# RMSNorm with swish on one core: 88 rows loaded ahead of the first store and 8 behind it, in place of 80 and 16

## The chip, the core and the metric

The kernel runs on one core of a Trainium2 chip. The time is what the device takes for one execution, in microseconds. Before the change it is 159.97 us, the median of 3 runs (159.83 to 160.32). The profile was taken in a run of 159.75 us, of which the profiled span, from the first instruction to the last landing, is 158.4 us.

## What is computed

The input is 16 x 1024 rows of 512 float32 numbers, 33.55 MB, and the output is as large. Each row is divided by its root mean square, multiplied by gamma, and put through the swish function:

```
rms = np.sqrt(np.mean(x ** 2, axis=-1, keepdims=True) + eps)
x_norm = x / rms * gamma
return (x_norm * (1.0 / (1.0 + np.exp(-x_norm)))).astype(np.float32)
```

## The kernel before

**Rows and groups.** Each of the 128 partitions handles 128 rows of 2 KB. In what follows "row" means such a row on every partition at once, so one row is 128 x 2 KB = 256 KB of traffic, and 128 rows are loaded and 128 stored. `groups = [32, 48, 16, 32]` says how rows are laid on the tensor in HBM: in a group of n rows every partition has n rows in one contiguous piece, so partitions lie n x 2 KB apart (64, 96, 32 and 64 KB). No load or store crosses a group's end.

**The ring.** `xb` holds 96 rows on each partition. Rows 0 to 95 have a place of their own; rows 96 to 127 reuse the places of rows 0 to 31, so their loads need the store of rows 0 to 31 to have landed. Everything is computed in place in `xb`.

**Loads and stores.** `loads` and `stores` are lists of (first row, number of rows), one DMA each. All are issued by SP (SyncE) on one hardware queue, which spreads each DMA over the core's 16 DMA engines, 8 partitions on each. `order` is the order in which SP issues them, written out by hand:

- loads at rows 0, 4, 8, then gamma, then loads at 16, 24, 32, 48, 64 (11 rows) and 75 (5 rows);
- `("landed", 64)`: SP waits until the load of rows 64 to 74 has landed (line 166);
- the store of rows 0 to 31, which itself waits for the swish of its four units (`s_swish`, lines 117 to 123), then the load of rows 80 to 95;
- `("stored", 0)`: SP waits until the store of rows 0 to 31 has landed, then issues the loads at 96, 112 (13 rows) and 125 (3 rows);
- `("landed", 112)`, then the stores at 32, 64, 80, 96 and 120, each on its swish.

**Compute.** Rows are worked in 16 units of 8 rows. ScalarE (ACT) squares and sums six rows of a unit (line 215), VectorE (DVE) the other two (line 251), GpSimd (POOL) turns the sums into 1/rms (lines 183 and 189), DVE scales the rows by it and by gamma (line 260), and ACT applies the swish to the whole unit in one instruction (line 225, and line 245 for the last two units). ACT's loop squares unit i + 2 and then does the swish of unit i, so a unit's swish waits behind the squares of a unit two later. TensorE multiplies nothing; its queue only passes on "this unit's load has landed" to ACT (`s_land`).

Of the kernel before, what the change touches and what calls it, by code (L numbers as in the profile page):

```python
# [9 lines left out]
def kernel(  # L10
# [14 lines left out]
    of = out.flatten_outer_dims()  # L25
    R, D = xf.shape

    groups = [32, 48, 16, 32]
    ring = 96
    loads = [(0, 4), (4, 4), (8, 8), (16, 8), (24, 8), (32, 16), (48, 16), (64, 11), (75, 5)]  # L30
    loads += [(80, 16), (96, 16), (112, 13), (125, 3)]
    stores = [(0, 32), (32, 32), (64, 16), (80, 16), (96, 24), (120, 8)]
    order = [("load", a) for a in (0, 4, 8)] + [("gamma", 0)]
    order += [("load", a) for a in (16, 24, 32, 48, 64, 75)]
    order += [("landed", 64), ("store", 0), ("load", 80)]
    order += [("stored", 0), ("load", 96), ("load", 112), ("load", 125)]
    order += [("landed", 112)] + [("store", a) for a in (32, 64, 80, 96, 120)]
    early = 2
    cn = 8
    own = 2  # L40
# [285 lines left out]
```

## Time and profile before

| What | Value |
|---|---|
| median of 3 runs | 159.97 us (159.83 to 160.32) |
| the profiled run | 159.75 us |
| its span | 158.4 us |
| traffic | 67.12 MB, 424 GB/s over the span |
| busy: ACT, DVE, POOL | 73%, 68%, 27% of the span |

The next table has all DMAs of `xb` in the order in which SP issued them: when SP issued each, when the last of its 16 engines had landed it (the issue plus the time to landing that the trace gives for it), and how long that is after the landing of the DMA ahead of it. All times are us from the span's start. Since the DMAs of the one queue land in order of issue, the last column is what each costs in line.

| DMA (rows) | issued | landed | after the one ahead |
|---|---|---|---|
| load 0 to 3 (4) | 0.00 | 4.95 | |
| load 4 to 7 (4) | 0.44 | 7.43 | 2.48 |
| load 8 to 15 (8), and gamma | 1.92 | 12.34 | 4.91 |
| load 16 to 23 (8) | 3.17 | 17.23 | 4.89 |
| load 24 to 31 (8) | 3.61 | 22.12 | 4.89 |
| load 32 to 47 (16) | 4.17 | 31.83 | 9.71 |
| load 48 to 63 (16) | 4.65 | 41.55 | 9.72 |
| load 64 to 74 (11) | 5.13 | 48.25 | 6.70 |
| load 75 to 79 (5) | 5.66 | 51.33 | 3.08 |
| store 0 to 31 (32) | 48.37 | 70.98 | 19.65 |
| load 80 to 95 (16) | 48.77 | 80.80 | 9.82 |
| load 96 to 111 (16) | 71.00 | 90.51 | 9.71 |
| load 112 to 124 (13) | 71.37 | 98.42 | 7.91 |
| load 125 to 127 (3) | 71.86 | 100.28 | 1.86 |
| store 32 to 63 (32) | 98.48 | 119.62 | 19.34 |
| store 64 to 79 (16) | 98.87 | 129.31 | 9.69 |
| store 80 to 95 (16) | 109.83 | 139.02 | 9.71 |
| store 96 to 119 (24) | 131.11 | 153.50 | 14.48 |
| store 120 to 127 (8) | 136.41 | 158.35 | 4.85 |

The landing of the last store is the end of the span.

### The profile page before, as it was taken

What the parts mean: (1) busy time and instruction counts of PE and PEld (TensorE: products, weight loads), DVE (VectorE), ACT (ScalarE), POOL (GpSimd) and SP (SyncE); (2) the same over time, 40 slices, a digit from 0 to 9 for tenths busy, and PEclk for the clock granted to TensorE, in tenths of its full rate; (3) what the DMA queues carried; (4) which work ended last, traced back from release to release, by engine and by line L of the source; (5) the groups of instructions that cost most, each with busy time, mean ns of one, the idle gap of its engine ahead of it and who ended that gap; (6) DMA issues with size and microseconds to landing.
All of it is one profiled execution on the core that took longest, in us unless ns stands there. A gap on an engine that the chain in (4) does not pass through costs nothing. (4 is left out here: it accounts for less than half of the span.)

```text
span 158.4 us, 844 instructions
## 1 busy us (share of the span) xinstructions
DVE 107.7 (68%) x198; ACT 115.7 (73%) x205; POOL 42.9 (27%) x38
## 2 busy tenths in 40 slices
DVE  0051899798989889898925989989898995000000
ACT  3608389999999999999459999999999385400000
POOL 1031426060524426060601433516061500000000
DMA  7999999999999979799999999996969999999997
GB/s 257 451 416 443 422 488 439 397 406 497 389 395 565 463 331 530 314 381 480 406 406 472 399 430 400 550 513 281 530 298 488 406 397 455 538 397 397 397 397 331
DMA packets 2744, 67.12 MB, mean 424 GB/s; under 512 B 308, under 2 KB 308, under 8 KB 440
## 3 DMA queue, kind: packets, MB, share of 16 engines
q1 hardware_dynamic: 2744, 67.12, 99.1%
HBM read 33.56 MB, written 33.55 MB: 424 GB/s over the span
## 5 line engine op out<-in xcount | busy, mean ns | idle before, releaser
L260 DVE SCALAR_TENSOR_TENSOR xb<-xb,rstd,gamma_sb 128x512 f32 (+1 forms) x128 | 86.1, 745 | 0.0
L215 ACT ACTIVATE junk<-xb 128x512 f32 (+1 forms) x94 | 54.6, 581 | 13.1 <-ACTq L98 11.3
L225 ACT ACTIVATE xb<-xb x14 | 50.5, 3604 | 0.7 <-ACTq L98 0.7
L251 DVE SCALAR_TENSOR_TENSOR junk_v<-xb 128x512 f32 (+1 forms) x34 | 22.1, 689 | 23.0 <-DVEq L98 23.0
L189 POOL TENSOR_TENSOR rstd<-aeps,neg_half 128x8 f32<-128x8 f32 x16 | 31.7, 1984 | 1.3
L183 POOL TENSOR_SCALAR aeps<-ms 128x8 f32<-128x8 f32 x16 | 10.4, 648 | 79.1 <-DVE junk_v L251 79.1
L215 ACT ACTIVATION_READ_ACCUMULATOR junk<-xb 128x1 f32 x94 | 17.7, 188 | 0.0
L245 ACT ACTIVATE xb<-xb 128x4096 f32<-128x4096 f32 x2 | 7.2, 3616 | 5.0 <-DVE xb L260 5.0
L251 DVE DVE_READ_ACCUMULATOR junk_v<-xb 128x1 f32 x34 | 2.8, 82 | 0.0
L227 ACT ACT_TABLE_LOAD x1 | 1.3, 1283 | 1.9 <-PEq L62 1.9
L269 DVE LOAD_MASK_SELECT gamma_sb<-gamma x1 | 0.0, 14 | 2.0 <-DMA gamma<-in_gamma_dram 2.0
L178 POOL MEMSET gamma<- 128x512 f32 x1 | 0.5, 524 | 1.5 <-POOLq L62 1.5
L269 DVE STREAM_SHUFFLE gamma_sb<-gamma 128x512 f32<-128x512 f32 x1 | 0.7, 719 | 0.0
L307 POOL MEMSET const-float32-0.0<- 128x1 f32 x1 | 0.1, 98 | 0.2 <-issue 0.2
L179 POOL MEMSET neg_half<- 128x8 f32 x1 | 0.1, 104 | 0.0
L307 POOL MEMSET const-bfloat16-1.0<- 128x1 bf16 x1 | 0.1, 103 | 0.0
L307 POOL MEMSET const-uint8-127<- 128x1 uint8 x1 | 0.1, 102 | 0.0
L307 POOL MEMSET const-float32-1.0<- 128x1 f32 x1 | 0.1, 99 | 0.0
## 6 DMA issues: line engine op xcount, KB each, us to landing
xb<-in_x_dram SPq DMA_DIRECT2D x4, 4096.0 KB, 29.9
out_dram<-xb SPq DMA_DIRECT2D x2, 4096.0 KB, 29.8
xb<-in_x_dram SPq DMA_DIRECT2D x3, 2048.0 KB, 14.1
out_dram<-xb SPq DMA_DIRECT2D x1, 6144.0 KB, 22.4
xb<-in_x_dram SPq DMA_DIRECT2D x1, 3328.0 KB, 27.0
xb<-in_x_dram SPq DMA_DIRECT2D x1, 2816.0 KB, 43.1
xb<-in_x_dram SPq DMA_DIRECT2D x2, 1024.0 KB, 6.0
out_dram<-xb SPq DMA_DIRECT2D x1, 2048.0 KB, 21.9
```

What stands on the lines that cost most here:

```text
L178: nc.gpsimd.memset(gamma4, 0.0).then_inc(s_zero, 1)
L179: nc.gpsimd.memset(neg_half, -0.5).then_inc(s_half, 1)
L183: nc.gpsimd.tensor_scalar(out=aeps[k % 2], in0=ms[min(k, 1)], scalar1=eps_f, scalar2=None, op0=ALU.add,),
L189: nc.gpsimd.tensor_tensor(out=rstd[:, k * cn : (k + 1) * cn], in0=aeps[k % 2], in1=neg_half, op=ALU.pow),
L215: nc.scalar.activation(out=dummies[j], in_=rows[j], func=AF.Square, scale=inv_d**0.5, accum_out=sums[:, j : j + 1],)
L225: nc.scalar.activation(out=rows, in_=rows, func=AF.Silu).then_inc(s_swish, 1)
L227: nc.scalar.preload_act_table_set("silu_and_others")
L245: nc.scalar.activation(out=rows, in_=rows, func=AF.Silu), s_norm, n + 1
L251: ins = nc.vector.scalar_tensor_tensor(out=junk_v[j], in0=rows[j], scalar=inv_d, in1=rows[j], op0=ALU.mult, op1=ALU.mult, accum_out=to[:, ...
L260: ins = nc.vector.scalar_tensor_tensor(out=rows[j], in0=rows[j], scalar=factors[j], in1=gamma_sb, op0=ALU.mult, op1=ALU.mult,)
L269: need(nc.vector.stream_shuffle(gamma_sb, gamma4, [0] * 32), s_gld, 16).then_inc(s_gamma, 1)
L307: nc = _bacc.Bacc("TRN2", target_bir_lowering=False, num_devices=1)
```

## The change

The groups become groups of 32, 56, 8 and 32 rows, so that partitions lie 64, 112, 16 and 64 KB apart. The two loads of rows 64 to 74 and 75 to 79 and the first half of the load of rows 80 to 95 become one load of 24 rows, 64 to 87; rows 88 to 95 are a load of 8 rows. The two stores of rows 64 to 79 and 80 to 95 become stores of 24 and 8 rows. SP no longer waits for the load at row 64 before the first store; the load behind that store is that of rows 88 to 95. There is one load fewer and the same number of stores. The instruction lists of DVE, ACT, POOL and TensorE are the same as before.

```
-    groups = [32, 48, 16, 32]
+    groups = [32, 56, 8, 32]
     ring = 96
-    loads = [(0, 4), (4, 4), (8, 8), (16, 8), (24, 8), (32, 16), (48, 16), (64, 11), (75, 5)]
-    loads += [(80, 16), (96, 16), (112, 13), (125, 3)]
-    stores = [(0, 32), (32, 32), (64, 16), (80, 16), (96, 24), (120, 8)]
+    loads = [(0, 4), (4, 4), (8, 8), (16, 8), (24, 8), (32, 16), (48, 16), (64, 24)]
+    loads += [(88, 8), (96, 16), (112, 13), (125, 3)]
+    stores = [(0, 32), (32, 32), (64, 24), (88, 8), (96, 24), (120, 8)]
     order = [("load", a) for a in (0, 4, 8)] + [("gamma", 0)]
-    order += [("load", a) for a in (16, 24, 32, 48, 64, 75)]
-    order += [("landed", 64), ("store", 0), ("load", 80)]
+    order += [("load", a) for a in (16, 24, 32, 48, 64)]
+    order += [("store", 0), ("load", 88)]
     order += [("stored", 0), ("load", 96), ("load", 112), ("load", 125)]
-    order += [("landed", 112)] + [("store", a) for a in (32, 64, 80, 96, 120)]
+    order += [("landed", 112)] + [("store", a) for a in (32, 64, 88, 96, 120)]
```

## The prediction

> **What bounds the kernel now.** I read the page's busy shares and DMA queue first, then SP's waits, then SP's and ACT's timelines around the first store, and last the time from issue to landing of each DMA (the table above).
>
> ```profile
> span 158.4 us, 844 instructions
> DVE 107.7 (68%) x198; ACT 115.7 (73%) x205; POOL 42.9 (27%) x38
> q1 hardware_dynamic: 2744, 67.12, 99.1%
> ```
>
> No compute engine is busy for three quarters of the span, while the packets of the one DMA queue fill 99.1% of all 16 DMA engines' time. The DMA queue is the bound, and the order of its DMAs is a line in which only two things can cost time: what each DMA takes in line, and a moment in which the line is empty.
>
> What a DMA takes in line is in the table's last column. A 16-row load takes 9.72 us, an 8-row load 4.89. Two of 8 cost 9.78, so one DMA more costs 9.78 - 9.72 = 0.06 us, and a row (9.72 - 0.06) / 16 = 0.604 us. A check with rows not used for this: 5 rows should take 0.06 + 5 x 0.604 = 3.08 (measured 3.08), 11 rows 6.70 (6.70), 24 rows 14.56 (14.48, a store). A change of direction costs a little more: store 0 took 19.65 against 19.34 for the other 32-row store, and the load behind it 9.82 against 9.72.
>
> Where the line could run empty is where SP waits with little queued. These are SP's waits:
>
> ```profile
> engine line waited for: us in total, times, longest us
> SPq L166 <- DMA xb<-in_x_dram: 68.3, 2, 42.1
> SPq L121 <- ACT xb L245: 25.9, 2, 20.9
> SPq L115 <- DMA out_dram<-xb: 21.8, 1, 21.8
> SPq L170 <- DMA out_dram<-xb: 21.6, 1, 21.6
> SPq L121 <- ACT xb L225: 10.5, 1, 10.5
> ```
>
> The two waits of line 166 are for the loads at rows 64 and 112; line 115's 21.8 us is the load at 96 waiting for store 0. Around them SP and ACT did this (start, duration):
>
> ```profile
> 3.17 2.94 SPq L115 DMA_DIRECT2D xb<-in_x_dram  x6
> 48.37 0.35 SPq L121 DMA_DIRECT2D out_dram<-xb  x1
> 48.77 23.53 SPq L115 DMA_DIRECT2D xb<-in_x_dram  x4
> 98.48 38.26 SPq L121 DMA_DIRECT2D out_dram<-xb  x5
> ...
> 44.75 3.60 ACT L225 ACTIVATE xb<-xb  x1
> 73.48 3.61 ACT L225 ACTIVATE xb<-xb  x1
> 80.96 0.60 ACT L215 ACTIVATE junk<-xb 128x512 f32 x1 [3.88 <-ACTq L98]
> 127.46 3.62 ACT L245 ACTIVATE xb<-xb 128x4096 f32<-128x4096 f32 x1 [3.30 <-DVE xb L260]
> ```
>
> I call the work still in line at an issue its cover (landing of the last DMA queued ahead, less the issue):
>
> - store 0: issued 48.37, load 75 lands 51.33: cover 2.96 us.
> - load 96: issued 71.00, load 80 lands 80.80: cover 9.80.
> - store 32: issued 98.48, load 125 lands 100.28: cover 1.80.
> - stores 64, 80, 96, 120: covers from 7.9 (131.11 to 139.02) to 29 us.
>
> The shortest cover, 1.80 us, still let store 32 take 19.34 in line, the shorter of the two 32-row stores. So no cover here has been short enough to add to the last landing.
>
> **The wait removed, and the store.** Unit 3's swish ends at 44.75 + 3.60 = 48.35; load 64 has landed at 48.25. Both end within 0.1 us and the swish is the later, so without the landed wait store 0 is still issued at 48.37. The removal alone is worth 0.0 us (at most 0.1 either way). Behind it on SP stand only the load at 88 and the loads of the ring's second round, which wait for the store's landing in any case.
>
> **Fewer loads in line.** Loads of rows 64 to 95 cost 6.70 + 3.08 + 9.82 = 19.60 us in line. Afterwards: 24 rows 0.06 + 24 x 0.604 = 14.56, and 8 rows behind a store 4.89 + 0.10 = 4.99, together 19.55. That is -0.05 us, one DMA fewer.
>
> **The stores re-cut.** 16 + 16 rows took 9.69 + 9.71 = 19.40; 24 + 8 rows, by the rows of stores 96 and 120, take 14.48 + 4.85 = 19.33. The number of DMAs is the same, so I take between 0 and -0.07: -0.03.
>
> **The two covers that move.** Load 64 (24 rows) lands at 41.55 + 14.56 = 56.11, so store 0's cover grows to 56.11 - 48.37 = 7.74 us. Store 0 lands at 56.11 + 19.65 = 75.76. Then SP issues load 96, with load 88 in line until 75.76 + 4.99 = 80.75: cover 4.99 us, where it was 9.80. What it needs: the very first load was issued into an empty line and landed 4.95 us later, of which 4 x 0.604 + 0.06 = 2.48 are transfer, so 2.47 are issue, start and landing receipt. 4.99 is twice that, and 2.8 times the 1.80 that sufficed at store 32: 0.0 us. If that cover did fail wholly, load 96 would take the 4.95 - 2.48 = 2.47 us more.
>
> The Trainium skill (DMA: Bandwidth & Descriptors, "Anatomy of one DMA") speaks against this edit: a DMA has about 2 us of fixed cost, mostly the receipt that the last byte has landed, slowest for writes to HBM. Store 0's receipt and load 96's first byte (0.6 us there) would by it use an estimated 2.6 of the 4.99 us. The line would still not run empty and the sum would be the same, but less would be to spare than the 1.80 at store 32 suggests.
>
> **Landed 112, and the compute.** Up to the load at 112 as many rows are in line as before (157), so store 32 is issued some 0.05 us earlier, with the same 1.8 us of cover. ACT no longer idles 3.88 us before unit 10, which now lands at 56.11; unit 11 lands at 80.75 and is wanted at 73.48 + 3.61 + 7.18 = 84.3 (7.18 is ACT's beat: 44.75 less 37.57, the starts of two swishes). From there ACT runs 3.9 us ahead of before: unit 10's swish ends at 98.6 (it was 102.6), unit 11's at 105.8, and stores 96 and 120 are issued at some 127 and 132.5. The line is then full for 12 us and more, so the gain ends in longer cover: 0.0 us. Were that cover gone, the end would follow ACT's last swish, which is now the earlier one.
>
> **The new layout.** Partitions lie 112 and 16 KB apart, which the trace does not show. At 96 KB (load 48) 16 rows took 9.72, at 64 KB (load 96) 9.71, at 32 KB (store 80) 9.71. I take 0.0; both bounds are by these rows: none gains over 9.69, so 0.1 us below; above, the worst difference among them, 0.1 per DMA, in 4 DMAs: 0.4 us.
>
> **Sum.** -0.05 - 0.03 = -0.08 us on a run of 159.75 us, so 159.67; the median of the runs shown lies 0.22 above the profiled run, so 159.9 us. About 0.3% (0.48 us) is what a measurement of this kernel can tell from no change, so this is no change.
>
> **Rival 1: load 96 comes too late (slower).** The place is SP's wait for store 0, the mechanism the cover of 8 rows. It decides once the time from store 0's last landing to load 96's first data exceeds what load 88 still has in line. The price is at most 2.47 us, halfway 1.2: 159.9 + 1.2 = 161.1. Against it stand the 1.80 us that sufficed at 98.48; for it, that the cover is halved and that all 16 engines must have landed the store first. Chance 0.08.
>
> **Rival 2: rows 64 to 95 move more slowly (slower).** 24-row pieces at 112 KB or 8-row pieces at 16 KB could suit HBM less, in two loads and two stores. To show, 64 rows (38.7 us in line) would need 1.3% more; at 2% it is 0.8 us: 160.7. For it there is only that no row has this layout; against it, three layouts within 0.1%. Chance 0.11.
>
> **Rival 3: the line runs empty before, in runs that were not profiled (faster).** Store 0's 2.96 us of cover hang on two events that fall within 0.1 us, and the runs spread over 0.49 us. If the median run loses 0.5 there and the new 7.74 us take that away, it is 159.4. Against it: the profiled run is within 0.14% of the median. Chance 0.13.
>
> The Trainium skill (SBUF — State Buffer, "The DMA setup-cost knee") has a rule that ends here too: some 2 us for every DMA, so one DMA fewer would give an estimated 157.9. The trace has 0.06 us between DMAs queued behind each other, so this has next to no part in the 0.13.
>
> **Chances and range.** No change 0.68; faster by over 0.3% 0.13; slower 0.19 (0.08 + 0.11). The range runs from rival 3's time with 0.1 to spare, 159.3, past rival 2's 160.7 to 160.8; rival 1's full price is left out.
>
> **What would show it.** In the profile after: store 0 issued at 48.4, landing near 75.8; load 96 issued just behind it and landing 9.7 us after load 88; ACT without a wait of over 1 us between 73 and 84; stores 24 and 8 taking 14.5 and 4.85 in line; a span of 158.3. A landing of load 96 more than 10 us behind load 88 would be rival 1; 24 rows over 14.7 us or 8 over 5.1 rival 2. An unchanged profile with a median below 159.5 would be rival 3.

## The result, and the profile after

| | before | after |
|---|---|---|
| median of 16 runs | 159.78 us | 160.37 us |
| lowest and highest | 159.53 to 160.32 | 160.04 to 160.72 |
| span of the profiled run | 158.4 us | 159.0 us |
| ratio of the times | | 1.0037, 95% interval 1.0028 to 1.0047 |

The change makes the kernel slower by 0.37%, about 0.6 us, just beyond what a measurement of it can tell from no change. The forecast was no change, 159.9 us.

The page of the changed kernel still shows a full DMA queue and compute engines with time to spare:

```profile
span 159.0 us, 842 instructions
DVE 107.7 (68%) x198; ACT 115.6 (73%) x205; POOL 42.8 (27%) x38
q1 hardware_dynamic: 2600, 67.12, 99.0%
```

The busy share of the queue does not show the loss: a packet that takes longer counts as busy. SP's timeline (start, duration):

```profile
3.17 2.36 SPq L115 DMA_DIRECT2D xb<-in_x_dram  x5
48.32 0.35 SPq L121 DMA_DIRECT2D out_dram<-xb  x1
48.71 28.98 SPq L115 DMA_DIRECT2D xb<-in_x_dram  x4
99.03 33.67 SPq L121 DMA_DIRECT2D out_dram<-xb  x5
```

The first store goes out at 48.32, as it did (48.37), but its turn in line is later. The second store goes out 0.55 us later than before (98.48). What lies between is read from the DMA issues (DMA, number, size, time from issue to landing):

```profile
xb<-in_x_dram SPq DMA_DIRECT2D x1, 6144.0 KB, 51.8
xb<-in_x_dram SPq DMA_DIRECT2D x1, 3328.0 KB, 22.2
xb<-in_x_dram SPq DMA_DIRECT2D x1, 768.0 KB, 23.5
```

The 6144 KB are the load of 24 rows: issued at 5.05, landed at 56.90. Put beside the table of the kernel before (last landings, us; only the rows around the change; the last column has the prediction's prices, and those of the kernel before where it gave none):

| DMA (rows) | issued | landed | after the one ahead | forecast |
|---|---|---|---|---|
| load 48 to 63 (16) | 4.57 | 41.50 | 9.70 | 9.72 |
| load 64 to 87 (24) | 5.05 | 56.90 | **15.40** | 14.56 |
| store 0 to 31 (32) | 48.32 | 76.40 | 19.50 | 19.65 |
| load 88 to 95 (8) | 48.71 | 81.32 | 4.92 | 4.99 |
| load 96 to 111 (16) | 76.42 | 91.03 | 9.71 | 9.71 |
| load 112 to 124 (13) | 76.79 | 98.94 | 7.91 | 7.91 |
| load 125 to 127 (3) | 77.26 | 100.80 | 1.86 | 1.86 |
| store 32 to 63 (32) | 99.03 | 120.19 | 19.39 | 19.34 |
| store 64 to 87 (24) | 99.41 | 134.76 | 14.57 | 14.48 |
| store 88 to 95 (8) | 105.78 | 139.59 | 4.83 | 4.85 |

One line is off: the load ahead of the first store takes 0.84 us too long. The DMA packets show where. Each engine moves this load in eight packets of 48 KB; seven take 1.82 us, and the eighth of all 16 engines, started between 53.2 and 53.8, takes 2.3 to 3.1 us. Nothing is idle then; the loads run slower for the last stretch ahead of the store.

### The profile page after: what moved, and what is told of

It is laid out like the page before. It is cut to its first block, busy times and chain, and to the rows that moved or that the text cites. A ratio compares the mean times of both kernels' runs of the same rounds, so it can differ in the third digit from the quotient of the medians.

```text
span 159.0 us, 842 instructions
## 1 busy us (share of the span) xinstructions
DVE 107.7 (68%) x198; ACT 115.6 (73%) x205; POOL 42.8 (27%) x38
## 5 line engine op out<-in xcount | busy, mean ns | idle before, releaser
L215 ACT ACTIVATE junk<-xb 128x512 f32 (+1 forms) x94 | 55.4, 589 | 9.1 <-ACTq L98 7.4
L215 ACT ACTIVATION_READ_ACCUMULATOR junk<-xb 128x1 f32 x94 | 18.5, 197 | 0.0
## 6 DMA issues: line engine op xcount, KB each, us to landing
xb<-in_x_dram SPq DMA_DIRECT2D x1, 6144.0 KB, 51.8
```

The costliest lines, as they stand in the source:

```text
L215: nc.scalar.activation(out=dummies[j], in_=rows[j], func=AF.Square, scale=inv_d**0.5, accum_out=sums[:, j : j + 1],)
```

## The experiments

Two numbers describe each run. The **cover** is what the first store has in line ahead of it when it is issued, at full speed (last landing of the load at 48, plus the in-line price of what follows, less the issue). The **loss** is what a stretch takes above its price in line (0.06 us for a DMA and 0.604 for a row), read from the mean landing of the 16 engines in the trace, since the last engine alone strays, by half a us in most runs and by up to 1.1: **ahead** for the loads from row 64 up to the store, **behind** for the first store and the load behind it. Each is of one profiled execution; the ratios are of the medians against the kernel before, with their 95% intervals. In some runs the profiled execution is not a typical one: it is 0.26 to 0.42 us slower than the median in b1, c3, c4, d3 and e2, and 0.31 faster in d4.

| run | store out | cover | loss ahead | loss behind | ratio |
|---|---|---|---|---|---|
| before | 48.37 | 2.96 | 0.0 | 0.15 | 1 |
| after | 48.32 | 7.74 | 0.76 | 0.08 | 1.0037 (1.0028 to 1.0047) |
| a1_tail5 | 48.26 | 7.78 | 0.66 | 0.03 | 1.0040 (1.0024 to 1.0055) |
| a2_layout64 | 48.15 | 7.74 | 0.80 | 0.0 | 1.0026 (1.0016 to 1.0037) |
| a3_before_one16 | 48.16 | 2.90 | 0.0 | 0.32 | 1.0011 (0.9998 to 1.0024) |
| a4_before_nowait | 48.25 | 2.96 | 0.0 | 0.10 | 1.0005 (0.9996 to 1.0014) |
| b1_tail5_landed | 52.91 | 2.98 | 0.08 | 0.06 | 0.9992 (0.9984 to 1.0001) |
| b2_tail10_landed | 49.88 | 6.03 | 0.84 | 0.04 | 1.0039 (1.0026 to 1.0052) |
| b3_tail8_landed | 51.00 | 4.82 | 0.99 | 0.09 | 1.0053 (1.0036 to 1.0069) |
| b4_behind_late | 48.00 | 7.75 | 1.04 | 0.0 | 1.0042 (1.0030 to 1.0054) |
| c1_store8first | 48.35 | 7.68 | 0.91 | 0.0 | 1.0034 (1.0022 to 1.0046) |
| c2_store2first | 48.25 | 7.69 | 0.77 | 0.03 | 1.0030 (1.0018 to 1.0042) |
| c4_tail3_landed | 54.20 | 1.81 | 0.0 | 0.75 | 1.0028 (1.0018 to 1.0038) |
| d4_tail7_landed | 51.80 | 4.23 | 0.50 | 0.07 | 1.0050 (1.0037 to 1.0062) |
| e1_before_early24 | 40.95 | 10.13 | 0.48 | 0.0 | 1.0019 (1.0010 to 1.0028) |
| e2_late_by_sum | 53.46 | 2.53 | 0.0 | 0.73 | 1.0016 (1.0007 to 1.0025) |

c3, d1, d2 and d3 are told below.

**First theory: the size of the last packets.** In the kernel before, the last load ahead of the store has packets of 10 KB; after, 48 KB.

a1_tail5, against after:

```diff
-    loads = [..., (48, 16), (64, 24)]
+    loads = [..., (48, 16), (64, 19), (83, 5)]
```

> The changed kernel with its load of 24 rows cut into 19 and 5 rows, nothing else. Theory T (the last packet of each engine ahead of the first store is slowed in proportion to its size, 0.91 us per engine for 48 KB packets, none for 10 KB): the time goes back to about 159.75 (ratio to before 0.999 to 1.001), and the DMA ahead of the store takes its 3.08 us in line. Theory Q (the store costs because it is issued 7.7 us ahead of its turn): no change against the changed kernel, ratio 1.0035 to 1.004, the loss now in the 5-row load or the 19-row load. Theory L (the layout with 112 KB pitch): also 1.0035 to 1.004.

1.0040. The size of the last packets is not it: the 10 KB packets are slow too. Theory T falls.

a2_layout64, against after:

```diff
-    groups = [32, 56, 8, 32]
+    groups = [32, 64, 32]
```

> The changed kernel's DMAs with groups of 32, 64 and 32 rows, so that partitions lie 128 KB apart in the third of the rows where it was 112 and 16 KB. T and Q: as the changed kernel, ratio to before 1.0035 to 1.004, with the load of 24 rows taking some 15.4 us in line. L: a different loss, below 1.002 or above 1.006.

1.0026, and the load of 24 rows took 15.61 us in line. The ratio is a little under the range of T and Q, but the loss is in the same place and of the same size with partitions 128 KB apart. The 112 and 16 KB are not needed for it.

a3_before_one16, against before:

```diff
-    loads = [..., (48, 16), (64, 11), (75, 5)]
+    loads = [..., (48, 16), (64, 16)]
...
-    order += [("landed", 64), ("store", 0), ("load", 80)]
+    order += [("store", 0), ("load", 80)]
```

> The kernel before with its two loads of 11 and 5 rows as one of 16, and so without the landed wait ahead of the first store; the store still goes out on its swish at 48.4. T: the last packets are of 32 KB, so a loss of about two thirds of 0.9 us in that load's landing, less what comes back behind the store: ratio 1.002 to 1.004. Q: the store is queued 2.9 us ahead as before, so no loss, ratio 0.999 to 1.001. L: no loss, 0.999 to 1.001.

1.0011 with an interval that holds 1, and no loss ahead of the store: the 16 rows took 9.72. This too speaks against T; the 0.3 us at the store's end is told of below.

a4_before_nowait, against before:

```diff
-    order += [("landed", 64), ("store", 0), ("load", 80)]
+    order += [("store", 0), ("load", 80)]
```

> The kernel before without the landed wait ahead of the first store, nothing else. T, Q and L alike: the store goes out on its swish at 48.4 as before, ratio 0.999 to 1.001. If the wait itself matters (a store put in line while the load of 11 rows is still landing), 1.002 or more.

1.0005, the same. In the kernel before, the wait itself is worth nothing, because the swish holds the store back as long.

**Second theory: the time at which the store is issued.** a1 cuts the stretch finely enough to see it in the windows view. The columns are the stretch, its length, busy times of DVE, ACT and POOL, the clock, the DMA share and the GB/s of the packets that start in it. a1_tail5:

```profile
53.50:54.00 0.50, 0.50 (x2) 0.50 (x1) 0.50 (x1) 1.00 1.10 348
54.00:54.50 0.50, 0.50 (x2) 0.50 (x1) 0.42 (x2) 1.00 1.38 328
54.50:55.00 0.50, 0.50 (x2) 0.50 (x1) 0.50 (x1) 1.00 0.78 184
```

The same stretch of b1_tail5_landed, which has the same DMAs and issues the store 4.65 us later:

```profile
53.50:54.00 0.50, 0.50 (x2) 0.50 (x1) 0.48 (x1) 1.00 0.98 410
54.00:54.50 0.50, 0.50 (x2) 0.50 (x1) 0.44 (x1) 1.00 0.97 389
54.50:55.00 0.50, 0.50 (x2) 0.50 (x1) 0.50 (x1) 1.00 1.02 430
```

The compute engines do the same work in both; the loads fall to 184 GB/s in one and hold 389 to 430 in the other. By the packets' own times, the loads of a1 run at some 0.55 of full speed between 54.3 and 55.2, before any packet of the store starts (the first at 55.8).

b1_tail5_landed, b2_tail10_landed and b3_tail8_landed, against after (19 and 5 rows shown; the others 14 and 10, 16 and 8):

```diff
-    loads = [..., (48, 16), (64, 24)]
+    loads = [..., (48, 16), (64, 19), (83, 5)]
...
-    order += [("store", 0), ("load", 88)]
+    order += [("landed", 64), ("store", 0), ("load", 88)]
```

> The changed kernel with loads of 19 and 5 rows in place of 24 and a landed wait for the load of 19 rows ahead of the first store: the store goes out at about 53.0 with 3.1 us of loads in line, where it went out at 48.3. Base: the same cut without the wait lost 0.64 us in line in the 5-row load (3.72 us in place of 3.08), its packets slow from 53.1 to 55.4. Theory I (loads are slowed some 4.8 us after a store was issued): the slow stretch falls at 57.8, where no load is in line, so no loss, ratio to before 0.999 to 1.001. Theory P (in the last 3 us ahead of the store's turn the engines already work on the store, if it is in line by then): it comes into line at 54, so half the loss or less, ratio 1.001 to 1.002. Theory N (the time of issue does not matter): 1.004.

> As the run with 19 and 5 rows and the wait, cut into 14 and 10 rows: the store goes out at about 50.1 with 6.1 us in line. I: the slow stretch starts at 54.9, part of the loss (0.2 to 0.5 us in the 10-row load), ratio 1.001 to 1.003. P: whole loss, slow from 53.1 to 55.4, ratio 1.004. N: 1.004.

> As the run with 19 and 5 rows and the wait, cut into 16 and 8 rows: the store goes out at about 51.2 with 4.9 us in line. I: the slow stretch starts at 56.0, when the loads are over, so no loss, ratio 0.999 to 1.001. P: whole loss, slow from 53.1 to 55.4, ratio 1.004. N: 1.004.

0.9992, 1.0039 and 1.0053. SP's timeline of b1:

```profile
52.91 0.35 SPq L120 DMA_DIRECT2D out_dram<-xb  x1
53.30 23.83 SPq L114 DMA_DIRECT2D xb<-in_x_dram  x4
```

With the store issued at 52.91 (cover 2.98) the loss is all but gone from 15 of the 16 engines; one engine still lands the 5 rows 0.6 us late, in a profile that is among the slowest of this kernel's runs (159.87, median 159.61), and why is not known. At 49.88 and 51.00 the loss is whole and begins at 53 as in the changed kernel. So it does not follow the issue at a fixed distance (theory I falls), and the issue matters (N falls). P fits best: the slow stretch lies in the last 3 us ahead of the store's turn, if the store is in line by then. Its forecast for b1, up to half the loss and 1.001 to 1.002, was missed all the same: next to nothing was lost.

b4_behind_late, against after:

```diff
-    order += [("store", 0), ("load", 88)]
+    order += [("store", 0), ("swished", 5), ("load", 88)]
...
+        elif what == "swished":
+            nc.sync.wait_ge(s_swish, a)
```

> The changed kernel with SP waiting for the swish of unit 4 (about 55.5) between the first store and the load of rows 88 to 95, so that only the store is in line behind the loads when they are slowed. I, P and N: as the changed kernel, ratio 1.0035 to 1.004, the load of 24 rows taking 15.4 us. If it is the load behind the store that disturbs the loads ahead: no loss there (14.55 us), ratio 0.999 to 1.001.

1.0042, with the loss ahead: it is the store in line that matters, not the load behind it.

c1_store8first and c2_store2first, against after (c1; c2 has 2 and 30 rows):

```diff
-    stores = [(0, 32), (32, 32), ...
+    stores = [(0, 8), (8, 24), (32, 32), ...
...
-    order += [("store", 0), ("load", 88)]
+    order += [("swished", 4), ("store", 0), ("store", 8), ("load", 88)]
```

> The changed kernel with its first store cut into 8 and 24 rows, both issued on the swish of unit 3 at 48.3 as before; SP then waits for both before the load at 96. Theory P1 (ahead of the store's turn the engines work on the store's first packet only, so the loads are at half rate for as long as that packet takes): the first packets are of 16 KB in place of 64, the stretch 0.6 us in place of 2.4, the load of 24 rows takes 14.56 + 0.23 = 14.8 us in line, ratio to before 1.0005 to 1.0015. Theory P2 (a given time or number of bytes ahead, whatever the packets): 15.4 us in line, ratio 1.004.

> As the run with 8 and 24 rows, with the first store cut into 2 and 30 rows, so first packets of 4 KB and 60 KB behind them. P1: next to no loss, 14.6 us in line for the load of 24 rows, ratio 0.9995 to 1.001. P2: 15.4 us, ratio 1.004 to 1.005.

1.0034 and 1.0030, with 15.57 and 15.38 us in line for the load of 24 rows: the loss does not depend on the first store's packets. P1 falls.

c3_before_no112, against before:

```diff
-    order += [("landed", 112)] + [("store", a) for a in (32, 64, 80, 96, 120)]
+    order += [("store", a) for a in (32, 64, 80, 96, 120)]
```

> The kernel before without the landed wait for the load at 112, nothing else: the 32-row store of rows 32 to 63 goes out at about 77 in place of 98.5, some 22 us ahead of its turn. If what was seen at the first store holds for any store in line behind loads (P1 and P2): the loads at 112 and 125 together take 0.6 to 1.0 us more than 9.76, ratio 1.003 to 1.006. If it is something of the first store alone: ratio 0.998 to 1.000, since the short idle time of the engines at 99 goes too.

1.0056 (1.0030 to 1.0083). The second store goes out at 76.85, some 22 us earlier than before, and the loads of 13 and 3 rows ahead of it lose 0.45 us in the mean and 1.2 on the last engine. The load of 3 rows landed 28.4 us after its issue before; now:

```profile
xb<-in_x_dram SPq DMA_DIRECT2D x1, 768.0 KB, 29.6
```

So the loss is not of the first store alone, and it shows what the wait for the load at 112 is worth in the kernel before: about 0.9 us.

**The time of issue alone.** In e2 all DMAs and their order are those of the changed kernel; SP waits for a count of DVE's that comes at 53.45. Against after:

```diff
-    order += [("store", 0), ("load", 88)]
+    order += [("summed", 7), ("store", 0), ("load", 88)]
...
+        elif what == "summed":
+            nc.sync.wait_ge(s_sum, a)
```

> The changed kernel with its DMAs as they are, in the same order; SP only waits, ahead of the first store, until DVE has the sums of unit 6, at about 53.45, so the store goes out at 53.5 with 2.6 us in line in place of 48.3 with 7.7. If the time of issue alone causes the loss: the load of 24 rows takes 14.5 to 14.6 us in line in place of 15.4, ratio to before 0.999 to 1.001 (up to 1.003 if the loss comes back behind the store, as with loads of 21 and 3 rows). If the single load of 24 rows takes part: 15.0 us or more, ratio 1.003 to 1.004.

SP's timeline of e2_late_by_sum, and then its load of 24 rows among the DMA issues:

```profile
53.46 0.35 SPq L120 DMA_DIRECT2D out_dram<-xb  x1
53.85 23.19 SPq L114 DMA_DIRECT2D xb<-in_x_dram  x4
```

```profile
xb<-in_x_dram SPq DMA_DIRECT2D x1, 6144.0 KB, 50.9
```

It lands 50.9 us after its issue in place of 51.8, 14.53 in line, the forecast price. The time of the store's issue alone made the difference ahead of it (the load at 88 goes out later too, but b4, with that load late and the store early, kept the loss). The time gains only part of that (1.0016): 0.73 us are lost behind the store, in a profile that is the slowest of e2's runs (160.53, median 160.11).

The two columns of loss do not add up to the time, because what the engines lie apart costs again later. In e2 the first and the last engine land the load at 88 1.57 us apart (0.92 in before). The second store is issued when all 16 have landed the load at 112, and those ahead run out of packets before its own come: by the packets' times the engines are busy for 0.4 of the time between 99.50 and 100.25, and the second store takes 0.50 us above its price in the mean, against 0.10 in before.

e1 does the reverse to the kernel before: it lets a part of the first store go out early.

```diff
-    stores = [(0, 32), (32, 32), ...
+    stores = [(0, 24), (24, 8), (32, 32), ...
...
-    order += [("landed", 64), ("store", 0), ("load", 80)]
+    order += [("store", 0), ("store", 24), ("load", 80)]
```

> The kernel before with its first store cut into 24 and 8 rows and no landed wait: the 24 rows go out on the swish of unit 2 at 41.2, 9 us ahead of their turn at 50.3, the loads and their cut (80 and 16 rows) as before. If the time of issue causes the loss: the loads of 11 and 5 rows lose 0.6 to 1.0 us between 47 and 50, ratio to before 1.003 to 1.005. If the cut into 88 and 8 rows is needed for it: 0.999 to 1.001.

1.0019 (1.0010 to 1.0028). The loads of 11 and 5 rows lose 0.48 us, between 49 and 51, ahead of a turn that lies 5 us earlier than in the changed kernel, and with the old cut into 80 and 16 rows. The ratio is under the range expected: the loss is smaller than the 0.6 to 1.0 us forecast, and the 0.15 us that the kernel before loses behind the store is not lost here.

**Where it sets in, and what comes back behind the store.** c4 and d4 differ from b1 in the rows of the last load ahead of the store, 3 and 7 in place of 5, and so in the cover.

> The changed kernel with loads of 21 and 3 rows in place of 24 and a landed wait for the load of 21 rows, so that the first store goes out at about 54.2 with 1.9 us in line, as the second store does with the loads of 13 and 3 rows. P1 and P2: no loss but up to 0.2 us of idle engines, ratio to before 0.998 to 1.000. If the idle time counts in full on the slowest engine: 1.001.

> The changed kernel with loads of 17 and 7 rows and a landed wait for the load of 17 rows: the store goes out at about 51.9 with 4.3 us in line, between the runs with 3.1 to 3.6 us (no loss) and 4.9 to 5.6 us (whole loss). If the loss sets in at once: ratio 1.004 or 0.999. If it grows with the cover: 1.001 to 1.003.

d4 (cover 4.23) loses 0.50 us ahead in its profile, the fastest of its six runs (160.07, median 160.38); by the ratio, 1.0050, a usual run of it loses as much as the kernels with longer covers. So the loss sets in between covers of 3.0 and 4.2 us (the expectation counts some of the covers larger; by the table's definition the runs on either side have 2.9 to 3.0 and 4.8 or more). c4 (cover 1.81) loses nothing ahead and 0.75 behind, 1.0028, which was not expected. Its last 64 KB packets of the store and the first packets of the load behind it are slow, as in e2.

The last attempt was to issue the loads behind the store late, too. d1 (on b1), d2 (on before) and d3 (on c4) cut the first store into 28 and 4 rows; SP waits for the 28, issues the loads at 88 (d2: 80) and 96, waits for the 4 and goes on:

```diff
-    stores = [(0, 32), (32, 32), ...
+    stores = [(0, 28), (28, 4), (32, 32), ...
...
+    order += [("landed", 64), ("store", 0), ("store", 28), ("stored", 0)]
+    order += [("load", a) for a in (88, 96)]
+    order += [("stored", 28), ("load", 112), ("load", 125), ("landed", 112)]
```

> The changed kernel with loads of 19 and 5 rows and the landed wait ahead of the first store (which alone gave ratio 0.9992), and the first store cut into 28 and 4 rows: the loads at 88 and 96 are issued when the 28 rows have landed, some 2.4 us ahead of their turn, in place of 22 us ahead. Theory S (the loss is the same for loads in line behind a store): the last packets of the store and the first of the load run at full rate, 0.15 us gained, 0.06 lost by one DMA more, ratio 0.998 to 0.9995. Theory O (only stores behind loads do this): ratio 0.999 to 1.0005.

> The kernel before with its first store cut into 28 and 4 rows and the loads at 80 and 96 issued when the 28 rows have landed. S: the 0.3 us that it loses around the end of the store are gone, less 0.06 for one DMA more: ratio 0.998 to 0.999. O: 1.000 to 1.001.

> The kernel with loads of 21 and 3 rows (ratio 1.0028, 0.8 us lost around the end of the first store, where its 64 KB packets starting at 72 took 0.59 us longer per engine) with the store cut into 28 and 4 rows and the loads at 88 and 96 issued when the 28 rows have landed. S: those 0.8 us are gone, ratio 0.998 to 0.9995. O: 1.002 to 1.004.

1.0060 (1.0043 to 1.0076), 1.0013 (1.0005 to 1.0022) and 1.0062 (1.0044 to 1.0081). Theory S falls: holding the loads back makes it worse, with losses behind the store of 0.57, 0.38 and 0.77 us and the last engine 1.2 to 1.8 us behind the first. Theory O fits d2 alone; d1 and d3 lie above its ranges as well. A store in line early slows the loads ahead of it; no run shows that a load in line early does the same to the store ahead of it.

## Why the prediction failed

**The step that failed** is the one on the covers that move: "Load 64 (24 rows) lands at 41.55 + 14.56 = 56.11, so store 0's cover grows to 56.11 - 48.37 = 7.74 us", entered in the sum with no price of its own. The cover did grow to 7.7 us, and that was the cost: the load of 24 rows took 15.40 us in line in place of 14.56, and 14.53 in e2, where the cover is 2.5 us. The step asked how short a cover may be and never whether it may be too long. The trace of before could have raised the question. Both of its stores behind loads had 1.8 and 3.0 us of cover; nothing in it showed a store that had been in line for longer with loads ahead of it, so that longer cover is free was an assumption with no row under it, and no bound was set for it.

**The wait removed.** "The removal alone is worth 0.0 us" is right of the kernel before (a4: 1.0005, interval from 0.9996). It was priced there and carried over to a line whose turn had moved by 5 us. In the new order the same wait, with a load to wait for that leaves 3 us, is worth the difference between a1 and b1, which differ in nothing else: 1.0040 and 0.9992.

**What held.** The store went out at 48.32 (forecast 48.37). Load 96 was issued 0.02 us behind the store's landing and landed 9.71 us behind load 88, so rival 1, too short a cover there, did not happen; the 5 us sufficed. The receipt of some 2 us that the prediction weighed took less: store 0's landings are counted some 0.7 us after the ends of its last packets. ACT's wait of 3.88 us is gone, and stores 96 and 120 went out at 127.06 and 132.36 (forecast 127 and 132.5) without any gain, since the line was full. Here is ACT after unit 7's swish, in the timeline, with no idle time in brackets:

```profile
73.41 3.62 ACT L225 ACTIVATE xb<-xb  x1
76.92 0.60 ACT L215 ACTIVATE junk<-xb 128x512 f32 x1
```

The stores re-cut took 14.57 + 4.83 = 19.40 us, as the two of 16 rows had; the gain of 0.03 entered for them was not there.

**Two readings that were off.** Neither moved the forecast. The covers of the last four stores reach 20.75 us (store 64: 98.87 to 119.62), not 29. And the prediction put the 19.65 us of store 0 against the 19.34 of store 32 down to a change of direction, but both stores follow loads; by the mean of the 16 landings they took 19.81 and 19.49.

**Rivals 2 and 3.** Rival 2 would have been called right by its own mark, "24 rows over 14.7 us", and is wrong: with the same layout the load takes 14.53 (e2), with another it takes 15.61 (a2). The mark named a place, not a cause. Rival 3 had the sign wrong; the kernel before loses nothing ahead of its first store.

**What stays open.** The runs show when the loads slow down, not what in the DMA engines or in HBM does it. Nor is it settled why the loss comes back behind the store with covers of 1.81 and 2.53 us (0.75 and 0.73) and hardly with 2.90 to 3.00 (0.06 to 0.32 in before, a3, a4, b1 and the first store of c3): seven points, in kernels that differ in more than the cover. That the time has a narrow best place near 3 us is what they suggest. No run beat the kernel before beyond its interval; b1 comes nearest, 0.9992 (0.9984 to 1.0001), and is the one to take if 88 and 8 rows are wanted.

## What to carry to other kernels

When a kernel is bound by one DMA queue, the moment at which a DMA is put in line has a price at both ends: too late and the line runs empty, but a store put in line 4 us or more ahead of its turn, behind loads, cost those loads 0.5 to 1.0 us here. A wait that looks idle in the profile, because another wait ends at the same moment, must be priced in the order that the change makes, not in the one it is taken from. And where an edit moves a quantity beyond the range that the trace shows, as the cover went from 3 to 7.7 us, the forecast needs a bound for it.

## What the runs showed of the hardware

- Loads with a store in line behind them slow down for some 2 us, to about 0.55 of full speed (a1, between 54.3 and 55.2), and most of it is over before the store's first packet starts. It came with covers of 4.23 us and more (nine runs and the changed kernel, 0.48 to 1.04 us lost, and the second store of c3, 0.45), and with 3.02 and less no more than 0.08 was lost in the mean of the engines. It came with packets of the loads of 10 to 48 KB and first packets of the store of 4 to 64 KB, with three layouts in HBM, and with and without a load in line behind the store.
- All 16 engines count as busy in that stretch, so the DMA share (99.0 and 99.1%) does not show it. What shows it is the landing of each DMA against that of the one ahead.
- A DMA more in a full line costs 0.06 us, and 24 rows in one load take the price worked out from 8 and 16 (14.53 for 14.56) when the store is issued 2.5 us ahead of its turn (e2).
- With a wait for all 16 engines, the distance between the first and the last becomes idle time of the others: 0.97 us at the second store of d3, with the engines 1.84 us apart, 0.50 in e2, with 1.57, and 0.10 in before, with 0.92.
